# An RMSNorm and matmul kernel on one core: x tiles ahead of the weights, x buffers of 8, 16 and 16 tiles, finer stores at the end

## The chip, the core and the metric

The kernel runs on one core of a Trainium2 chip. The metric is the time of one execution on the device in microseconds (us), the median of several runs. A profile is one further execution with the hardware profiler on; its span, from the first to the last instruction, is some 1.8 us shorter than the time. An execution can be disturbed and then count as slow (over 1.5% above the fastest of its kernel); of a single run that cannot be told, so its state is called unknown. Ratios are the mean time of one kernel's fast runs over the mean of the other's fast runs of the same rounds, so they are not quite the ratios of the medians quoted.

## The reference

```python
def setup_inputs():
    batch, seq, dim, out_dim = 16, 1024, 512, 768
    # x: (16, 1024, 512) f32, gamma: (512,) f32, weight: (512, 768) f32, eps = 1e-5

def reference(x, gamma, weight, eps):
    rms = np.sqrt(np.mean(x ** 2, axis=-1, keepdims=True) + eps)
    x_norm = x / rms * gamma
    return np.matmul(x_norm, weight).astype(np.float32)
```

The 16,384 rows are 128 tiles of 128 rows. A tile is 0.262 MB of x in and 0.393 MB of output out.

## The kernel before

For each tile GpSimd casts x to bf16, TensorE transposes it as two float32 words (two transposes of 128x128), VectorE copies the transposes out of PSUM, TensorE multiplies by the weights (four products of 768 columns, each as 512 and 256), ScalarE squares x for the norm, and ScalarE and VectorE in turn scale the result by 1/rms on its way out. SyncE issues all loads and stores in one queue, in program order. gamma is multiplied into the weights once.

```python
    XG, OG = 16, 8
    AHEAD = 20
    ...
    opening = [1, 1, 1, 1, 2, 2]
    last = NT // OG - 1
    x_first, x_size = stretches(XG, {0: opening + [4, 4], 1: [4, 4, 8], 2: [8, 8]})
    o_first, o_size = stretches(OG, {0: opening, 1: [4, 4], last - 1: [4, 4], last: [2, 2, 1, 1, 1, 1]})
    ...
    xin = ctx.enter_context(tc.tile_pool(name="xin", bufs=2))       # two buffers of 16 tiles of x
    outp = ctx.enter_context(tc.tile_pool(name="out", bufs=3))      # three buffers of 8 tiles of output
    ...
        load_weights(0)          # first half of the weights
        load_until(3)            # x tiles 0, 1, 2
        load_weights(1)          # second half
        load_until(2 * XG)       # the rest of 32 tiles
    ...
        warm_up(6)               # idle matmuls
        ...                      # gamma turned by TensorE
        weights(0, nc.vector, 0, WIDE)
        weights(0, nc.vector, WIDE, O)
        weights(1, nc.scalar)
        warm_up(7)
        for i in range(3):
            cast(i, nc.gpsimd)
            square(i, ssq[:, i:i + 1])
        transpose_tile(0)
        transpose_tile(1)
        matmuls(0, acc[0], [0, 1])
        warm_up(3)
        transpose_tile(2)
        matmuls(1, acc[1], [0, 1])
        matmuls(2, acc[2], [0, 1])
        weights(2, nc.vector)    # needs the second half
        ...
        weights(3, nc.scalar)
        ...
        matmuls(0, acc[0], [2, 3])
        finish_tile(0, acc[0], nc.scalar)
    ...
        for j in range(2, NP):                       # pairs of tiles
            load_until(2 * j + AHEAD)
            ...                                      # cast of pair j + 3, squares and transposes of pair j + 2
            for i, engine in ((2 * j, nc.scalar), (2 * j + 1, nc.vector)):
                a = accumulator()
                matmuls(i, a, range(K), feed)
                finish_tile(i, a, engine)            # scales, and stores when a stretch is full
```

## Time and profile before

| | before |
|---|---|
| time, median of the first 3 runs | 210.98 us (210.57 to 211.02) |
| span of the profile | 209.0 us |
| TensorE busy | 201.6 us, 96% of the span |
| TensorE's last product ends | 203.1 us |
| last store issued, landed | 203.9 us, 208.0 us |
| moved | 85.7 MB, mean 410 GB/s |

Two answers of the profile belong together here. First, of the instructions of one line (the two stores of the last tile), how long from issue to landing, minimum, median and maximum:

```profile
DMA to landing us min/median/max: 4.1/4.1/4.1
```

Second, of the waits of SyncE's queue, the one at the program's end (waiter, releaser, total us, times, longest):

```profile
SPq L344 <- DMA out_dram<-ot: 3.5, 1, 3.5
```

So the program's last 3.5 us are a wait for stores that were all issued before. The lines of the opening and the sums over stretches stand in the prediction.

### The profile page before, as it was taken

The page shows a single profiled execution, that of the slowest core. Times are in us where ns is not written, and L with a number is a line of the kernel's source. Part 1 is how long each engine was busy: PE and PEld are TensorE (multiplying, and loading weights), DVE is VectorE, ACT ScalarE, POOL GpSimd, SP SyncE. Part 2 cuts the span into 40 slices and gives each one's busy share as a digit, 9 for nine tenths or more (in the row PEclk, how much of TensorE's full clock was granted, in tenths as well). Part 3 has the DMA queues.
Part 4 walks back from the last instruction along what each step waited for, and adds up shares of the span by engine and source line. Part 5 has one row for each costly group of instructions (what it writes and reads, how often), then busy time and mean ns, then how long its engine had stood idle before and what let it go on. Part 6 is the DMA issues. An engine that isn't in the chain of part 4 may idle for free.

```text
span 209.0 us, 3534 instructions
## 1 busy us (share of the span) xinstructions
PE 201.6 (96%) x1298; PEld 137.9 (66%) x1298; DVE 109.0 (52%) x173; ACT 149.6 (72%) x359; POOL 67.0 (32%) x73
## 2 busy tenths in 40 slices
PE   7999999999999999999999999999999999999980
PEld 2466777666766776667766776667667766677640
DVE  0465654654565465456545644654564465456550
ACT  2689987787778778777877777787777778777640
POOL 1357532306331073213623062310633045230000
PEclk9999999999999999999999999999999999999999
DMA  6999999999999999999999999999999999899994
GB/s 231 392 430 422 408 395 436 424 414 439 431 458 411 412 442 425 447 411 437 428 448 419 423 423 442 433 433 417 428 442 447 405 441 414 381 386 386 383 374 182
DMA packets 7077, 85.69 MB, mean 410 GB/s; under 512 B 786, under 2 KB 916, under 8 KB 3476
## 3 DMA queue, kind: packets, MB, share of 16 engines
q1 hardware_dynamic: 7056, 85.46, 97.0%
q8 instruction: 10, 0.16, 0.3%
q14 instruction: 7, 0.06, 0.1%
q10 hardware_dynamic: 4, 0.00, 0.0%
HBM read 35.13 MB, written 50.33 MB: 409 GB/s over the span
## 4 chain that ended last, share of the span: by engine, by line
PE 91%; ACT 3%; DMA 2%; POOL 1%; DVE 1%; issue 0%; SPq 0%
PE ops L168 77%; PE tp L133 13%; DMA xt<-in_x_dram 2%; ACT jk L98 1%; ACT ot L150 1%; POOL xb L94 1%; ACT rms L102 0%; DVE xT L140 0%; PE ops L227 0%; DVE ot L152 0%; SPq L206 0%; DVE rstd L104 0%
## 5 line engine op out<-in xcount | busy, mean ns | idle before, releaser
L168 PE MATMUL ops<-w_bf,xT 128*128 128x256 bf16 (+1 forms) x1024 | 194.2, 326 | 0.3 <-DVE xT L140 0.3
L168 PEld LDWEIGHTS <-xT 128*128 128x128 bf16 x1024 | 100.0, 98 | 56.4 <-DVE xT L140 1.4
L94 POOL CAST xb<-xt 128x1024 bf16<-128x1024 f32 (+1 forms) x67 | 66.3, 1002 | 118.9 <-PE tp L133 72.9
L150 ACT ACTIVATE ot<-ops,rstd 128x768 f32<-128x768 f32 (+1 forms) x65 | 58.1, 894 | 47.2 <-PE ops L168 47.2
L140 DVE COPY xT<-tp 128x1024 bf16<-128x1024 bf16 (+1 forms) x67 | 44.7, 667 | 83.3 <-PE tp L133 83.0
L98 ACT ACTIVATE jk<-xt 128x512 bf16<-128x512 f32 x128 | 78.7, 619 | 0.7 <-DMA xt<-in_x_dram 0.7
L133 PE MATMUL tp<-ident_f,xb 128*128 128x128 f32 x256 | 68.9, 273 | 0.1
L152 DVE TENSOR_SCALAR ot<-ops,rstd 128x768 f32<-128x768 f32 (+1 forms) x65 | 64.5, 993 | 2.9 <-PE ops L168 2.9
L133 PEld LDWEIGHTS tp<-ident_f,xb 128*128 128x128 f32 x256 | 35.9, 141 | 3.8 <-POOL xb L94 0.7
L98 ACT ACTIVATION_READ_ACCUMULATOR jk<-xt 128x1 f32 x128 | 24.4, 191 | 0.0
L102 ACT ACTIVATE rms<-ssq,eps_sb 128x4 f32<-128x4 f32 (+3 forms) x35 | 10.4, 297 | 1.1
L104 DVE RECIPROCAL rstd<-rms 128x4 f32<-128x4 f32 (+3 forms) x35 | 5.9, 167 | 3.3 <-ACT rms L102 3.3
L227 PE MATMUL ops<-warm 128*128 128x512 bf16 x16 | 6.4, 561 | 1.2 <-DVE eps_sb L220 1.2
L227 PEld LDWEIGHTS <-warm 128*128 128x128 bf16 x16 | 1.9, 131 | 3.9 <-issue 2.5
L150 ACT ACTIVATE w_bf<-w_f,g_sb 128x768 bf16<-128x768 f32 x2 | 1.9, 936 | 3.6 <-DMA w_f<-in_weight_dram 3.6
L201 ACT ACT_TABLE_LOAD x1 | 1.3, 1283 | 1.3 <-PEq L330 1.3
L152 DVE TENSOR_SCALAR w_bf<-w_f,g_sb 128x512 bf16<-128x512 f32 (+2 forms) x3 | 1.4, 485 | 1.1 <-DMA w_f<-in_weight_dram 1.0
L241 DVE COPY g_sb<-tp 128x4 f32<-128x4 f32 x1 | 0.2, 162 | 3.1 <-PE tp L239 3.1
L239 PEld LDWEIGHTS tp<-ident_f,g_row 2*128 2x128 f32 x2 | 0.3, 200 | 0.8 <-issue 0.8
L218 DVE MEMSET warm<- 128x256 uint32 x1 | 0.3, 272 | 0.9 <-PEq L330 0.9
L239 PE MATMUL tp<-ident_f,g_row 2*128 2x2 f32 x2 | 0.4, 264 | 0.0
masks.py:199 POOL TENSOR_SCALAR_AFFINE_SELECT ident_f<-ident_f 128x128 f32<-128x128 f32 x1 | 0.3, 292 | 0.1
(6 smaller groups left out, 0.7 us busy)
## 6 DMA issues: line engine op xcount, KB each, us to landing
out_dram<-ot SPq DMA_DIRECT2D x12, 3072.0 KB, 16.3
xt<-in_x_dram SPq DMA_DIRECT2D x5, 4096.0 KB, 23.0
xt<-in_x_dram SPq DMA_DIRECT2D x3, 2048.0 KB, 19.4
out_dram<-ot SPq DMA_DIRECT2D x4, 1536.0 KB, 11.6
xt<-in_x_dram SPq DMA_DIRECT2D x4, 1024.0 KB, 13.2
out_dram<-ot SPq DMA_DIRECT2D x4, 768.0 KB, 10.4
out_dram<-ot SPq DMA_DIRECT2D x7, 384.0 KB, 11.2
w_f<-in_weight_dram SPq DMA_DIRECT2D x2, 768.0 KB, 5.9
```

Of the source, the lines that this page charges most:

```text
L94: engine.tensor_copy(out=xb_tiles[i // 2][:, i % 2:i % 2 + n, :], in_=held(x_tiles, XG, i, n))
L98: nc.scalar.activation(out=jk, in_=held(x_tiles, XG, i)[:, 0, :], func=AF.Square, accum_out=ssq)
L102: nc.scalar.activation(out=rms[:, :n], in_=ssq[:, :n], func=AF.Sqrt, scale=1.0 / D, bias=eps_sb)
L104: nc.vector.reciprocal(out=rstd[:, :n], in_=rms[:, :n])
L133: nc.tensor.transpose(out=tp_tiles[j][:, t, h, :], in_=words[:, lo:lo + P], identity=ident_f)
L140: nc.vector.tensor_copy(out=dst[:, t:t + n, :], in_=src[:, t:t + n, :])
L150: nc.scalar.mul(out=dst, in_=src, mul=r)
L152: nc.vector.tensor_single_scalar(out=dst, in_=src, scalar=r, op=mybir.AluOpType.mult)
L168: nc.tensor.matmul(out=acc[:, lo:hi], lhsT=xT_tiles[i // 2][:, i % 2, k // 2, :, k % 2], rhs=w_bf[:, k, lo:hi], start=(k == 0), stop=(k == ...
L201: nc.scalar.preload_act_table(AF.Sqrt)
L227: nc.tensor.matmul(out=spare[:, :WIDE], lhsT=warm[:, :P], rhs=warm, start=True, stop=True)
L239: nc.tensor.transpose(out=gp[:, c, :], in_=g_row[:, :, c], identity=ident_f[:2, :2])
```

## The change

The intent is to have the first x tiles cast and transposed by the time the weights come, to read further ahead (40 tiles in place of 32), and to let the stores of the last 24 tiles start earlier in smaller pieces. The diff, cut to its core:

```diff
-    XG, OG = 16, 8
+    OG = 8
...
+    groups = [8] + [16] * 7 + [8]
+    base = [sum(groups[:g]) for g in range(len(groups))]
...
-    opening = [1, 1, 1, 1, 2, 2]
+    opening = [1, 2, 1, 2, 2]
...
-    x_first, x_size = stretches(XG, {0: opening + [4, 4], 1: [4, 4, 8], 2: [8, 8]})
-    o_first, o_size = stretches(OG, {0: opening, 1: [4, 4], last - 1: [4, 4], last: [2, 2, 1, 1, 1, 1]})
+    x_first, x_size = stretches(groups, {0: opening, 1: [4, 4, 8]})
+    o_first, o_size = stretches([OG] * (last + 1), {0: opening, 1: [4, 4], last - 2: [4, 4], last - 1: [2, 2, 2, 2],
+                                 last: [2, 2, 1, 1, 1, 1]})
...
+    xin_first = ctx.enter_context(tc.tile_pool(name="xin_first", bufs=1))
     xin = ctx.enter_context(tc.tile_pool(name="xin", bufs=2))
...
+        touched = singles.tile([P, 2, 1], F32)
+        nc.scalar.dma_start(out=touched, in_=wv[:, :, 0:1])
...
-        load_weights(0)
-        load_until(3)
-        load_weights(1)
-        load_until(2 * XG)
+        load_until(3)
+        for h in range(2):
+            nc.sync.dma_start(out=w_f32[:, 2 * h:2 * h + 2, :].rearrange("p c o -> p (c o)"), in_=wv[:, h, :])
+        load_until(base[3])
...
         warm_up(6)
+        cast(0, nc.vector)
+        square(0, ssq[:, 0:1])
...
+        transpose_tile(0)
+        warm_up(3)
+        cast(1, nc.vector)
+        cast(2, nc.gpsimd)
...
+        transpose_tile(1)
+        transpose_tile(2)
+        warm_up(6)
...
-        warm_up(7)
...
-        warm_up(3)
...
+        for k in (0, 1):
+            for i in range(3):
+                matmuls(i, acc[i], [k])
```

More of the change, by code (lines that the diff above doesn't have):

```diff
@@ L37, with stretches @@
     NP = NT // 2
-    XG, OG = 16, 8
+    OG = 8
     AHEAD = 20
     WIDE = 512
-    def stretches(group, parts):
+    groups = [8] + [16] * 7 + [8]
+    base = [sum(groups[:g]) for g in range(len(groups))]
+    group_of = [g for g, n in enumerate(groups) for _ in range(n)]
+    def stretches(sizes, parts):
         first, size, i = {}, {}, 0
-        for g in range(NT // group):
-            for n in parts.get(g, [group]):
+        for g, whole in enumerate(sizes):
+            for n in parts.get(g, [whole]):
                 for t in range(i, i + n):
@@ L53, in stretches @@
         return first, size
-    opening = [1, 1, 1, 1, 2, 2]
+    opening = [1, 2, 1, 2, 2]
     last = NT // OG - 1
-    x_first, x_size = stretches(XG, {0: opening + [4, 4], 1: [4, 4, 8], 2: [8, 8]})
-    o_first, o_size = stretches(OG, {0: opening, 1: [4, 4], last - 1: [4, 4], last: [2, 2, 1, 1, 1, 1]})
+    x_first, x_size = stretches(groups, {0: opening, 1: [4, 4, 8]})
+    o_first, o_size = stretches([OG] * (last + 1), {0: opening, 1: [4, 4], last - 2: [4, 4], last - 1: [2, 2, 2, 2],
+                                 last: [2, 2, 1, 1, 1, 1]})
     def rows(ap, i, n):
-        if i < XG:
+        g = group_of[i]
+        if g == 0:
             return ap[i * P:(i + n) * P, :].rearrange("(p t) d -> p t d", t=n)
-        return ap.rearrange("(g p t) d -> g p t d", p=P, t=XG)[i // XG, :, i % XG:i % XG + n, :]
+        whole = ap[base[g] * P:(base[g] + groups[g]) * P, :].rearrange("(p t) d -> p t d", t=groups[g])
+        return whole[:, i - base[g]:i - base[g] + n, :]
     singles = ctx.enter_context(tc.tile_pool(name="singles", bufs=1))
+    xin_first = ctx.enter_context(tc.tile_pool(name="xin_first", bufs=1))
     xin = ctx.enter_context(tc.tile_pool(name="xin", bufs=2))
@@ L75, with x_held, o_held @@
     x_tiles, xb_tiles, tp_tiles, rstd_of, xT_tiles, o_tiles, norm_sums = {}, {}, {}, {}, {}, {}, {}
-    def held(tiles, group, i, n=1):
-        return tiles[i // group][:, i % group:i % group + n, :]
+    def x_held(i, n=1):
+        g = group_of[i]
+        return x_tiles[g][:, i - base[g]:i - base[g] + n, :]
+    def o_held(i, n=1):
+        return o_tiles[i // OG][:, i % OG:i % OG + n, :]
     def load(i):
-        if i // XG not in x_tiles:
-            x_tiles[i // XG] = xin.tile([P, XG, D], F32, name="xt")
-        nc.sync.dma_start(out=held(x_tiles, XG, i, x_size[i]), in_=rows(x, i, x_size[i]))
+        g = group_of[i]
+        if g not in x_tiles:
+            x_tiles[g] = (xin if g else xin_first).tile([P, groups[g], D], F32, name="xt")
+        nc.sync.dma_start(out=x_held(i, x_size[i]), in_=rows(x, i, x_size[i]))
     starts = [i for i in range(NT) if x_first[i] == i]
@@ L93, in cast @@
             xb_tiles[i // 2] = xbp.tile([P, 2, D], BF16, name="xb")
-        engine.tensor_copy(out=xb_tiles[i // 2][:, i % 2:i % 2 + n, :], in_=held(x_tiles, XG, i, n))
+        engine.tensor_copy(out=xb_tiles[i // 2][:, i % 2:i % 2 + n, :], in_=x_held(i, n))
     def square(i, ssq):
         jk = junk.tile([P, D], BF16, name="jk")
-        nc.scalar.activation(out=jk, in_=held(x_tiles, XG, i)[:, 0, :], func=AF.Square, accum_out=ssq)
+        nc.scalar.activation(out=jk, in_=x_held(i)[:, 0, :], func=AF.Square, accum_out=ssq)
     def root(i, n, ssq):
@@ L164, in store @@
         if i == first + n - 1:
-            nc.sync.dma_start(out=rows(out, first, n), in_=held(o_tiles, OG, first, n))
+            nc.sync.dma_start(out=rows(out, first, n), in_=o_held(first, n))
     def matmul(i, k, acc, lo, hi):
@@ L200 @@
         nc.scalar.dma_start(out=g_row, in_=gamma.rearrange("(h w c) -> h w c", w=P, c=2))
+        wv = weight.rearrange("(h w c) o -> w h (c o)", w=P, c=2)
+        touched = singles.tile([P, 2, 1], F32)
+        nc.scalar.dma_start(out=touched, in_=wv[:, :, 0:1])
         nc.scalar.preload_act_table(AF.Sqrt)
-        wv = weight.rearrange("(h w c) o -> w h (c o)", w=P, c=2)
+        load_until(3)
         w_f32 = singles.tile([P, K, O], F32)
-        def load_weights(h):
+        for h in range(2):
             nc.sync.dma_start(out=w_f32[:, 2 * h:2 * h + 2, :].rearrange("p c o -> p (c o)"), in_=wv[:, h, :])
-        load_weights(0)
-        load_until(3)
-        load_weights(1)
-        load_until(2 * XG)
+        load_until(base[3])
         for _ in range(20):
@@ L241 @@
         nc.vector.tensor_copy(out=g_sb, in_=gp)
+        transpose_tile(0)
+        warm_up(3)
+        cast(1, nc.vector)
+        cast(2, nc.gpsimd)
+        square(1, ssq[:, 1:2])
+        square(2, ssq[:, 2:3])
+        transpose_tile(1)
+        transpose_tile(2)
+        warm_up(6)
         acc = [accumulator() for _ in range(4)]
@@ L245 @@
         weights(1, nc.scalar)
-        warm_up(7)
-        for i in range(3):
-            cast(i, nc.gpsimd)
-            square(i, ssq[:, i:i + 1])
-        transpose_tile(0)
-        transpose_tile(1)
-        matmuls(0, acc[0], [0, 1])
-        warm_up(3)
-        transpose_tile(2)
-        matmuls(1, acc[1], [0, 1])
-        matmuls(2, acc[2], [0, 1])
+        for k in (0, 1):
+            for i in range(3):
+                matmuls(i, acc[i], [k])
+        root(0, 3, ssq)
         weights(2, nc.vector)
-        root(0, 3, ssq)
         weights(3, nc.scalar)
@@ L262 @@
         finish_tile(0, acc[0], nc.scalar)
+        transpose_tile(3)
+        norms(3, 1)
         matmuls(1, acc[1], [2, 3])
-        transpose_tile(3)
         finish_tile(1, acc[1], nc.vector)
-        norms(3, 1)
         cast(4, nc.gpsimd)
```

## The prediction

> **What bounds the kernel now.** I read the page first (busy shares and slices), then the chain that ended last, then the waits of the engines and of the DMA queue, then sums over stretches, and last the timeline of the opening and of the tail.
>
> ```profile
> PE 201.6 (96%) x1298; PEld 137.9 (66%) x1298; DVE 109.0 (52%) x173; ACT 149.6 (72%) x359; POOL 67.0 (32%) x73
> ...
> GB/s 231 392 430 422 408 395 436 424 414 439 431 458 411 412 442 425 447 411 437 428 448 419 423 423 442 433 433 417 428 442 447 405 441 414 381 386 386 383 374 182
> ...
> PE 91%; ACT 3%; DMA 2%; POOL 1%; DVE 1%; issue 0%; SPq 0%
> ```
>
> TensorE is busy 96% of the span and is 91% of the chain, but the transfers run at over 400 GB/s in nearly every slice too. Two resources are nearly full at once. The sums over stretches show where TensorE is not full:
>
> ```profile
> 0.00:4.00 4.00, 2.81 (x8) 0.88 (x8) 0.28 (x2) 1.28 (x1) 0.70 (x6) 1.00 0.52 190
> 4.00:6.50 2.50, 2.50 (x8) 1.05 (x9) 0.91 (x3) 1.09 (x2) 0.49 (x1) 1.00 1.08 356
> 6.50:9.30 2.80, 2.72 (x16) 1.43 (x15) 0.85 (x2) 2.07 (x7) 1.36 (x3) 1.00 1.01 403
> 9.30:11.60 2.30, 2.30 (x15) 1.19 (x13) 1.13 (x3) 0.97 (x3) 0.61 (x1) 1.00 1.03 421
> 11.60:21.00 9.40, 9.13 (x61) 6.19 (x60) 5.87 (x12) 8.93 (x23) 6.39 (x8) 1.00 1.02 427
> 21.00:203.20 182.20, 182.14 (x1199) 127.17 (x1196) 99.52 (x152) 135.00 (x327) 57.45 (x56) 1.00 0.99 421
> 203.20:209.00 5.80, 0.00 (x0) 0.00 (x0) 0.46 (x1) 0.23 (x1) 0.00 (x0) 0.91 0.53 203
> ```
>
> The columns are the stretch, its length, busy time of TensorE, its weight loads, VectorE, ScalarE and GpSimd, then clock, DMA share, GB/s. From 21.0 to 203.2 TensorE idles 0.06 us in 182. In the timeline one tile takes 60.69 to 62.21 = 1.52 us there. One tile moves 0.262 MB in and 0.393 MB out, so TensorE's pace demands 0.655 MB / 1.52 us = 431 GB/s, which is about what the slices show. So only the first 11 us and the last 6 us can give anything; the middle gives nothing unless a wait appears in it. The opening hangs on the weights:
>
> ```profile
> 5.41 0.94 ACT L150 ACTIVATE w_bf<-w_f,g_sb 128x768 bf16<-128x768 f32 x1 [2.83 <-DMA w_f<-in_weight_dram]
> ...
> 8.24 0.61 POOL L94 CAST xb<-xt 128x512 bf16<-128x512 f32 x1 [0.98 <-DMA xt<-in_x_dram]
> ...
> 10.07 0.94 ACT L150 ACTIVATE w_bf<-w_f,g_sb 128x768 bf16<-128x768 f32 x1 [0.75 <-DMA w_f<-in_weight_dram]
> 10.07 0.62 DVE L152 TENSOR_SCALAR w_bf<-w_f,g_sb 128x768 bf16<-128x768 f32 x1
> ```
>
> The first weight half is there at 5.4 us, x tile 0 at 6.0, tile 2 at 8.2, the second half at 10.07; the scaled second half exists at 11.0, and tile 0 is finished at 11.59.
>
> **What the skill says.** (1) "DMA: Bandwidth & Descriptors", Specifications, gives a fabric ceiling of 435 GB/s and an HBM limit of about 358 GB/s per core. The trace agrees with the first (best long stretches about 430 GB/s) and contradicts the second (421 GB/s over 182 us). (2) The same page, Issuing engines are not separate DMA queues: transfers issued from several engines run on the same 16 engines and interleave. So the new transfer on ScalarE's queue takes its turn among those of x. (3) "TensorE: Matmul & The Clock Gate", Part 1, says that the array starts at half rate until a window of about 3.4 us was busy, and that the window is free-running. The trace agrees: idle matmuls start 0.43 us apart up to 6.3 us and 0.21 us apart at 8.4 us; its clock record steps up at 6.6 us.
>
> **The change part by part.**
>
> *Order of the first loads.* Before: weight half, three tiles, weight half. After: tile 0, tiles 1 and 2 in one transfer, both halves. Ahead of the last byte of the second half lie the same 2 x 0.786 + 3 x 0.262 = 2.36 MB. Scaling and the last two products of tiles 0 to 2 need that half, so its landing decides, and it moves only by efficiency: one transfer fewer to issue (about 0.5 us of queue time, but the engines are already fed), packets of 4 KB at 25.7 GB/s per engine in the trace where single tiles have 2 KB at 21.8 GB/s on average, slowed by a patch of poor packets at 4.5 to 6.5 us (313 to 357 GB/s). Restoring 400 GB/s in that patch saves about 0.4 us; the 256 four-byte pieces that touch the weights may cost some 0.1 us. I take 9.7 us for the landing in place of 10.04.
>
> *What TensorE can do before.* After, tile 0 may land at about 3.6 us, tiles 1 and 2 at 5, the first half at about 7.7. The six transposes (0.11 us each) are then out of the way. First half scaled on VectorE (0.48 + 0.27) and ScalarE (0.94): first product at about 8.3, and the twelve products (3 tiles x 2 x 0.32 us = 1.9 us) are done at 10.2. Then TensorE waits for the second half: 9.7 + 0.62 = 10.3 (VectorE), 9.7 + 0.94 = 10.65 (ScalarE); tile 0 ends at about 11.0, against 11.59. So the start is worth 0.5 us, not the 2 us by which tile 0 comes earlier.
>
> *Idle matmuls.* 6 + 3 + 6 = 15 against 16; they fill the wait for weights and cost nothing unless still at half rate: six at 0.43 are 2.6 us, from 6.3 to 8.9, which would push the first product 0.6 us but be absorbed by the wait for the second half (to about 0.3).
>
> *x buffers.* 8 tiles once, then 16 and 16: 40 tiles issued ahead instead of 32. Later a buffer of 16 is refilled when its last tile is squared, as before, only 8 tiles shifted. In the steady part the lead is unchanged. The last refill before took 22.9 us and was issued at 147.0; GpSimd waited 7.84 us for it and cast at 170.08, some 2 us ahead of TensorE's need. I expect the same lead. Early on, stores queue behind 2.1 MB more loads (4.9 us at 430 GB/s); tile 24's output buffer needs tiles 0 to 7 stored, about 37 us before, 42 after, and is asked for at 47. Hidden.
>
> *Tail.* Stores of 104 to 119 go from 8, 4, 4 tiles to 4, 4, 2, 2, 2, 2. The last eight tiles are stored as before. In the trace the last 13 or so of 16 engines pause at about 181, 193 and 199.7 us (0.4 to 1 us each) for want of a store, but three engines, some 5 us behind at 181, never pause and carry the last landing: stores issued from 199.2 on land 0.9 us apart up to 207.98. So filling the pauses helps the engines that don't matter. From the store at 196.2 on, the two programs have the same stores. Gain: 0 to 0.3 us, given back in part by smaller packets (6 KB against 12 and 24 KB: about 2% of 0.2 MB per engine at 26 GB/s, some 0.15 us).
>
> Sum: TensorE's end moves from 203.1 to about 202.6; of that the slow engines let through about 0.4 us. 210.98 - 0.4 - 0.1 = **210.5 us**.
>
> **The rivals.**
>
> *A. The tail is set by the queue, not TensorE.* For it: landings 0.9 us apart at the end. Then a start 0.5 us earlier is lost wholly in a longer queue: 211.0.
>
> *B. The pauses of the DMA engines in the tail count after all,* that is, the slow engines are slow through sharing and gain when stores come sooner; then the last landing comes 1 to 2 us sooner, 209 to 209.5. Against: their packets take the same 0.91 us while others pause.
>
> *C. A new wait in the middle:* the demand of 431 GB/s is all that the transfers give, so a load of 16 tiles coming 2 us later than the 2 us of lead would stall TensorE, perhaps twice: 212 to 214. Against: the lead in the steady part is worked out as unchanged, and in the early part grows to some 4 us.
>
> *D. The clock steps up later,* as the idle matmuls have gaps in which the array waits for tiles 0 to 2: up to 2 us of products at half rate, 1 us: 211.5.
>
> **Range and chances.** A and D push up by up to 1 us, B down by 1.5, and the start may be off by 0.4 either way. Range 209.3 to 211.5. Two per cent is 4.2 us: the ends that the trace shows hold only about 11 + 6 us in all, most of it needed for the first 2.4 MB and the last store, so faster by that needs things that I do not see (2%); slower needs C repeated (2%).
>
> **What would show it.** Right: second weight half landing at 9.4 to 10.1; first product at 8.0 to 9.0, tile 0 finished at about 11.0; TensorE idle under 0.5 us from 21 us to its end at about 202.6; tile pace 1.52 us; last landings still about 0.9 us apart with TensorE's end 4 to 5 us ahead of the span's. Wrong: a wait of the transposes for GpSimd's casts in the middle (C), products over 0.4 us long after 8.5 us (D), a span that ends under 5 us after TensorE (B), or one that does not move though TensorE ends sooner (A).

## The result and the profile after

In the same rounds the kernel before took 210.87 us (210.57 to 211.02, 6 runs) and the changed one 210.86 us (210.60 to 211.46, 6 runs). The ratio is 1.0003, with a 95% interval of 0.9988 to 1.0019: the same. The changed kernel's result is correct.

The opening came out at the times worked out (by what, is taken up below). From the timeline of the changed kernel (start, duration, engine, line, operation, what ended the idle time before):

```profile
7.55 0.94 ACT L163 ACTIVATE w_bf<-w_f,g_sb 128x768 bf16<-128x768 f32 x1 [1.38 <-DMA w_f<-in_weight_dram]
...
8.10 2.81 PE L181 MATMUL ops<-w_bf,xT 128*128 128x512 bf16 x16
...
9.37 0.94 ACT L163 ACTIVATE w_bf<-w_f,g_sb 128x768 bf16<-128x768 f32 x1 [0.70 <-DMA w_f<-in_weight_dram]
9.37 0.62 DVE L165 TENSOR_SCALAR w_bf<-w_f,g_sb 128x768 bf16<-128x768 f32 x1 [0.49 <-DMA w_f<-in_weight_dram]
...
10.95 0.90 ACT L163 ACTIVATE ot<-ops,rstd 128x768 f32<-128x768 f32 x1 [0.64 <-PE ops L181]
```

The second half of the weights is there at 9.37 us, not 10.07, and tile 0 is finished from 10.95, not 11.59. The gain is 0.64 us, and it is kept to TensorE's end, as the sums over stretches show (stretch, length, busy time of TensorE, its weight loads, VectorE, ScalarE, GpSimd, then clock, DMA share, GB/s):

```profile
180.00:190.00 10.00, 9.89 (x67) 7.03 (x67) 5.33 (x9) 6.97 (x18) 2.60 (x3) 1.00 0.99 418
190.00:202.50 12.50, 12.45 (x80) 8.00 (x78) 6.51 (x10) 7.47 (x16) 0.00 (x0) 1.00 0.88 359
202.50:209.00 6.50, 0.01 (x1) 0.00 (x0) 0.49 (x1) 0.30 (x1) 0.00 (x0) 0.90 0.49 188
```

TensorE ends at 202.5 (before: 203.1). In this trace 25 product records are missing, so the busy times of the first two rows are a little low; no wait is recorded there. But the same two views of the end as before read:

```profile
DMA to landing us min/median/max: 4.6/4.6/4.6
```

```profile
SPq L360 <- DMA out_dram<-ot: 3.9, 1, 3.9
```

The last store is issued 0.63 us sooner (203.25 against 203.88) and takes 0.5 us longer to land (4.58 against 4.10), so it lands 0.16 us sooner. What TensorE saved at the start was given back as a longer wait for stores at the end.

### The profile page after: what moved, and what is told of

Same layout as the page of the kernel before. It is cut to its first block, busy times and chain, and to the rows that moved or that the text cites. A ratio compares the mean times of both kernels' runs of the same rounds, so it can differ in the third digit from the quotient of the medians.

```text
span 208.8 us, 3508 instructions
## 1 busy us (share of the span) xinstructions
PE 199.8 (96%) x1272; PEld 138.1 (66%) x1297; DVE 109.9 (53%) x175; ACT 149.6 (72%) x359; POOL 65.5 (31%) x71
## 4 chain that ended last, share of the span: by engine, by line
PE 91%; DMA 3%; DVE 1%; ACT 1%; issue 1%; SPq 0%; DVEq 0%
PE ops L181 78%; PE tp L146 13%; DMA w_f<-in_weight_dram 3%; DVE ot L165 1%; ACT ot L163 0%; SPq L96 0%; ACT jk L111 0%; DVE w_bf L165 0%; DVE xT L153 0%; ACT rms L115 0%; DVE rstd L117 0%; DVEq L165 0%
## 5 line engine op out<-in xcount | busy, mean ns | idle before, releaser
L181 PE MATMUL ops<-w_bf,xT 128*128 128x512 bf16 (+1 forms) x999 | 192.5, 324 | 1.4
L107 POOL CAST xb<-xt 128x1024 bf16<-128x1024 f32 (+1 forms) x65 | 64.8, 1015 | 119.8 <-DMA xt<-in_x_dram 61.6
L239 PE MATMUL ops<-warm 128*128 128x512 bf16 x15 | 5.7, 530 | 1.2 <-DVE eps_sb L232 1.2
L107 DVE CAST xb<-xt 128x512 bf16<-128x512 f32 x2 | 0.9, 467 | 2.4 <-DMA xt<-in_x_dram 2.4
```

What stands on the lines that cost most here:

```text
L107: engine.tensor_copy(out=xb_tiles[i // 2][:, i % 2:i % 2 + n, :], in_=x_held(i, n))
L181: nc.tensor.matmul(out=acc[:, lo:hi], lhsT=xT_tiles[i // 2][:, i % 2, k // 2, :, k % 2], rhs=w_bf[:, k, lo:hi], start=(k == 0), stop=(k == ...
L239: nc.tensor.matmul(out=spare[:, :WIDE], lhsT=warm[:, :P], rhs=warm, start=True, stop=True)
```

## The experiments

Theory Q: the 16 transfer engines set the end. At least one of them has work queued from 2 us to the last landing, so TensorE has slack at its end, and moving TensorE moves nothing until the slack is used up. Rival P: TensorE sets the end, and a fixed landing follows it. All kernels below are variants of the changed one; unless said, they give the correct result. In the texts of what was expected, 210.86 us is the time of the changed kernel.

A table of what the profiles showed. "Weights" is the landing of the second half, "TensorE" the end of its last product, "issue" and "land" those of the last store that has a recorded landing:

| kernel | weights | TensorE | issue | land | landing less issue | time, median |
|---|---|---|---|---|---|---|
| before | 10.04 | 203.14 | 203.88 | 207.98 | 4.1 | 210.87 |
| changed | 9.35 | 202.51 | 203.25 | 207.82 | 4.6 | 210.86 |
| late_7 | 9.85 | 204.53 | 205.27 | 208.45 | 3.2 | 211.24 |
| late_19 | 8.75 | 206.69 | 207.43 | 210.08 | 2.7 | 212.46 |
| less_products | 9.07 | 197.32 | 199.01 | 208.26 | 9.2 | 210.74 |
| no_store_48 | 9.88 | 203.01 | 203.33 | 205.98 | 2.7 | 208.59 |
| old_start | 10.07 | 203.16 | 203.90 | 208.25 | 4.4 | 210.96 |
| old_tail | 9.89 | 203.05 | 203.79 | 208.27 | 4.5 | 210.69 |

### TensorE later: late_7 and late_19

```diff
         for j in range(2, NP):
...
+            if j == 30:
+                idle = accumulator()
+                for _ in range(7):        # 19 in late_19
+                    nc.tensor.matmul(out=idle[:, :WIDE], lhsT=warm[:, :P], rhs=warm, start=True, stop=True)
```

> The changed kernel with 7 idle matmuls (7 x 0.216 = 1.5 us of TensorE) put before tile 60. Theory Q (the transfers set the end; TensorE has slack at the end): the last store is issued 1.5 us later (about 204.8 in place of 203.25) but lands at about the same time as in the changed kernel (207.8), issue to landing shrinking from 4.6 to about 3.1 to 3.4 us; time 210.9 to 211.2. Rival P (TensorE's end plus a fixed landing sets the end): time 212.3, issue to landing still 4.6 us.

> The same with 19 idle matmuls (4.1 us). Theory Q: the slack is the 4.6 us from issue to landing less an unloaded landing of some 2.3 us (estimate from the first x tile, 2.7 us with its slow first packets), so about 2 us; beyond it the time follows TensorE: 210.86 + 4.1 - 2.1 = 212.9 us. Rival P: 215.0 us.

late_7 measured 211.24 us, ratio to the kernel before 1.0017 (1.0002 to 1.0032); late_19 212.46 us, ratio 1.0081 (1.0065 to 1.0097). In late_19's profile TensorE ended 4.2 us later than in the changed kernel's and the span grew by 2.3 us (211.1 against 208.8); the median time grew by 1.6 us, less than the 2.0 us expected. The issue to landing of the last store shrank, first in late_7, then in late_19:

```profile
DMA to landing us min/median/max: 3.2/3.2/3.2
```

```profile
DMA to landing us min/median/max: 2.7/2.7/2.7
```

Rival P wanted 212.3 and 215.0 us and a landing of 4.6 us in both. It falls. Where the queue has drained, a last store lands in 2.7 us, so of the changed kernel's 4.6 us some 1.9 us are queue: that is TensorE's slack. The completions of the last store, one from each of the 16 transfer engines, say the same: in the changed kernel they run from 205.69 to 207.82 us, in late_19 from 209.85 to 210.08. The lag of the slowest engine is gone there.

### TensorE sooner: less_products

The fourth product of tiles 108 to 123 is left out; the result is wrong. (The line that marks the last product of a sum is changed to match, and is cut here.)

```diff
...
         for k in ks:
+            if 108 <= i < 124 and k == K - 1:
+                feed and feed()
+                continue
             matmul(i, k, acc, 0, WIDE)
```

> The changed kernel with the fourth of the four products left out for tiles 108 to 123 (a wrong result on purpose): 16 x 0.32 = 5.1 us less on TensorE, every transfer kept. Theory Q: TensorE ends at about 197.4 in place of 202.5, the last landing stays within 0.5 us of 207.8, issue to landing of the last store grows from 4.6 to about 9.5 us; time 210.4 to 210.9. Rival P: time about 205.8 us.

The time was 210.74 us, ratio to the kernel before 0.9997 (0.9982 to 1.0012). TensorE ended 5.2 us sooner, and the last store landed 0.4 us later. The sums over stretches of this run say it in two rows:

```profile
190.00:197.40 7.40, 7.32 (x47) 4.43 (x44) 4.51 (x8) 3.90 (x9) 0.00 (x0) 1.00 1.01 421
197.40:209.30 11.90, 0.00 (x0) 0.00 (x0) 0.45 (x1) 0.21 (x1) 0.00 (x0) 0.67 0.55 220
```

TensorE has nothing to do for the last 11.9 us of this span, while 220 GB/s x 11.9 us = 2.6 MB are still moved, and the span is no shorter. A TensorE that is faster by 5 us is worth nothing here.

### Fewer bytes: no_store_48

The store of tiles 48 to 55 is left out (3.1 MB); the result is wrong.

```diff
-        if i == first + n - 1:
+        if i == first + n - 1 and first != 48:
```

> The changed kernel without the store of tiles 48 to 55 (3.1 MB, some 7.3 us of transfer; a wrong result on purpose), TensorE's work kept. Theory Q: the queue is empty at the end, the last store lands about 2.3 to 2.7 us after its issue in place of 4.6, time about 208.9 us; TensorE's end stays at 202.5. Rival P: no change, 210.9 us.

The time was 208.59 us, ratio 0.9887 (0.9866 to 0.9908). TensorE ended at 203.0 us, 0.5 us later than in the changed kernel's profile and not at the 202.5 expected, since the second half of the weights landed 0.5 us later (9.88 us). Its slices of GB/s (40 slices of the span) show the hole where the store is missing, and lower rates before the end than in the changed kernel (295 GB/s from 190 us to 203 against 359 from 190 us to 202.5):

```profile
GB/s 220 401 429 443 433 386 382 433 451 451 409 422 441 433 424 420 441 425 436 443 123 427 357 455 332 427 435 460 406 428 420 441 419 438 403 422 359 253 316 279
```

```profile
DMA to landing us min/median/max: 2.7/2.7/2.7
```

The hole is at about 104 us, 100 us ahead of the end, and takes 2.3 us off the time. 3.1 MB are some 7.3 us of transfer, but the gain stops where TensorE and the 2.7 us of an unloaded landing set the end. With the late runs this bounds the matter from both sides: the transfers are ahead of TensorE as the bound by about 2 us in 211, and a kernel whose queue has drained at the end would take about 208.6 us (an estimate: the median of this run) as long as TensorE ends where it does.

### The parts undone: old_start, old_tail, no_touch

old_start puts back the opening of the kernel before (order of loads, no touch, casts on GpSimd, its idle matmuls). old_tail puts back its stores of tiles 104 to 119. no_touch drops only the 256 four-byte reads.

```diff
 # old_tail
-    ... 1: [4, 4], last - 2: [4, 4], last - 1: [2, 2, 2, 2],
+    ... 1: [4, 4], last - 1: [4, 4],
                                  last: [2, 2, 1, 1, 1, 1]})
 # no_touch
-        touched = singles.tile([P, 2, 1], F32)
-        nc.scalar.dma_start(out=touched, in_=wv[:, :, 0:1])
```

> The changed kernel with the opening of the kernel before (first weight half, three x tiles, second half; no touch; casts on GpSimd); buffers and tail stay changed. Theory Q: TensorE's end goes back by about 0.6 us to 203.1, the time stays within 0.3 us of 210.9. Rival P (TensorE's end sets the time): +0.6 us against the changed kernel. Further, if the opening alone moves the second weight half, it lands at about 10.0 us again.

> The changed kernel with the stores of the kernel before in the tail (tiles 104 to 119 by 8, 4, 4). Theory Q with the slowest engines never pausing: the last landing stays within 0.3 us of 207.8, time 210.6 to 211.2. Rival B of the prediction (pauses of the other engines count): the last landing 0.5 us or more later.

> The changed kernel without the 256 four-byte reads of the weights. If the reads help, the first and second weight half land later than 7.46 and 9.35 us (by some 0.4 us, the patch of poor packets at 2.5 to 3.5 us returning later); if they only cost, earlier by 0.1 to 0.4 us. In either case the time stays at 210.9 within 0.4 us.

old_start: 210.96 us, ratio to the kernel before 1.0006 (0.9991 to 1.0021); its weights landed at 10.07 and TensorE ended at 203.16, back where the kernel before had them. old_tail: 210.69 us, ratio 0.9990 (0.9973 to 1.0007). Neither part moves the time by anything that these runs can tell from zero. In old_tail the last landing was 208.27 us, 0.45 us later than in the changed kernel's profile, between what the two theories wanted; but no_store_48 apart, last landings of kernels with the new tail reach 208.26 as well, so one profile does not decide this, and the times do not favour the new tail.

no_touch had its two halves at 8.00 and 9.93 us, time 210.83 us in its single run. Later than the changed kernel's 7.46 and 9.35, as if the touch helped; but late_7, no_store_48 and old_tail, which have the touch, show 9.85 to 9.89. Over the eleven profiles with the new order and the touch the second half was in use from 8.8 to 10.2 us. What the touch is worth stays open; it is within that spread, and hidden by the slack at the end.

### Do the 16 engines lag alike? probe_engines and probe_high

A transfer reports 16 completions, one for each engine, and the trace has their times. In the changed kernel the store of tiles 88 to 95 (issued at 143.96) reported its eighth completion at 162.01 us and its last three at 163.07, 164.71 and 164.75. So two engines run 2.7 us behind the middle one. The first lag is a small one from the start (0.8 us at 17 us). It stepped to 2.3 us between 17 and 22 us, when one 16 KB instruction fetch, at 21.4 us, took 1.10 us of some engine; a step of 0.7 to 1.6 us is at that time in 12 of the 14 profiles (not in no_touch and shift_4), but no run here removes the fetch, so its part in the lag is not shown. By 175 us the slowest is 4.2 us behind, and it catches up only while the others pause in the tail, to 2.1 us at the end. In less_products the last store's eighth completion came at 203.6 us and its last at 208.26: there too the middle engine was done 4.6 us before the last, and the late ones set the end.

To find which engines lag, the store of one tile was cut so that its pieces can use few engines. The Trainium skill, "DMA: Bandwidth & Descriptors", section Why a DMA increments its semaphore by 16 and not by 1, says that a store issued from SyncE uses the largest number of engines up to 16 that divides its slowest dimension, and the lowest-numbered ones. The trace agrees on the number: after one update of its semaphore (the counter that the engines raise) at its issue, a piece of n partitions of those up to 15 showed n more, and the piece of 84 partitions in probe_high showed 14. Which engines they are rests on the page alone.

```diff
...
+        if i == 96:
+            a = 0
+            for m in list(range(1, 16)) + [8]:        # probe_high: (8, 10, 12, 14, 84)
+                nc.sync.dma_start(out=rows(out, i, 1)[a:a + m, 0, :], in_=out_tile(i)[a:a + m, :])
+                a += m
...
```

(The stores of tiles 96 to 103 are split into 1 and 7 tiles for this. The expectations count the engines from 0, so their engine 4 is the fifth.)

> The changed kernel with the store of tile 96 cut into 15 stores of 1, 2, ... 15 partitions and one of 8, so that the store of n partitions can use n engines at most. If a few fixed engines lag by some 4 to 5 us (theory Q's slow engines), the landings go up in steps: small up to the number of the first slow engine, then a jump of 2 us or more, and flat after the slowest one. If the lag moves from engine to engine, or all lag alike, the landings rise evenly (some 0.1 to 0.3 us each). Time within 0.5 us of 210.9.

> The changed kernel with the store of tile 96 in pieces of 8, 10, 12, 14 and 84 partitions (on at most 8, 10, 12, 14 and 14 engines), followed by the 7 other tiles on 16. Every piece holds engine 4, so if engine 4 is a fixed slow one, each of the pieces ends with one landing some 3 to 4 us after the others; a second late landing that first appears in the n-th piece tells of a second slow engine among those added. If the slow engine changes from run to run, the piece of 8 may show none. Time 210.9 within 0.5 us, as five stores do not fill the queue as sixteen did.

The pieces of 1, 2, 3, 4, 5, 6 and 7 partitions had their last completions at 167.95, 169.34, 169.56, 169.79, 173.18, 173.37 and 173.56 us. The jump of 3.4 us comes with the fifth piece, and the other completions of the later pieces stayed below 170.6. So in this run one engine, the fifth, was behind, and the first four, the sixth and the seventh were not. The probe spoiled its own second half: the program has eight completion semaphores in turn, with eight stores unlanded SyncE issued nothing more from 165.7 to 173.0 us, and by then the lag was gone; the load queued behind came late, and the run (a single one, state unknown) took 217.36 us instead of the expected 211. In probe_high (212.55 us in its single run, again more than expected) the piece of 8 partitions had completions from 167.89 to 173.92 us, the last one 2.7 us after the one before it. That agrees with the fifth engine but tells no number. One more can be read there: the whole store before the pieces had two late completions, at 173.48 and 173.69 us; the pieces of 8, 10 and 12 partitions have only one completion after 173.48, the piece of 14 has two (173.63 and 174.53). So, by the same numbering, the second late engine of that run is the thirteenth or the fourteenth.

### Bytes moved off the late engine: shift_4, shift_8, shift_16

If a late engine among numbers 5 to 16 sets the end, giving part of its bytes to the first four should shorten the run.

```diff
-            nc.sync.dma_start(out=rows(out, first, n), in_=o_held(first, n))
+            cuts = [(0, 112), (112, 116), (116, 120), (120, 124), (124, 128)] if first == 48 else [(0, P)]
+            for lo, hi in cuts:
+                nc.sync.dma_start(out=rows(out, first, n)[lo:hi], in_=o_held(first, n)[lo:hi])
```

(shift_4 has stores of 4 tiles at 48 to 55 and cuts the first; shift_16 cuts those at 48 and 64.)

> The changed kernel with one store of 8 tiles (48 to 55) cut into one of 112 partitions (7 for each of 16 engines) and four of 4 partitions (24 KB to each of engines 0 to 3 alone). Engines 0 to 3 get 4 x 0.91 - 0.91 = 2.7 us more to move, each of the others 0.91 us less. Theory Q, with the end set by a slow engine that is not among 0 to 3 (the first probe found engine 4 some 4 us behind, 0 to 3 and 5, 6 not): the last landing comes about 0.9 us sooner (206.9 in place of 207.8 to 208.2), since engines 0 to 3 take most of their 2.7 us out of pauses in the tail; time about 210.0. If the end were set by all engines alike, or by TensorE: 210.9 or above.

> The same with a store of 4 tiles cut: engines 0 to 3 get 1.4 us more, the others 0.46 us less. Theory Q: last landing about 0.45 us sooner, time about 210.4. Otherwise 210.9.

> The same with two stores of 8 tiles cut: engines 0 to 3 get 5.5 us more, the others 1.8 us less. Theory Q: engines 0 to 3 now are the slow ones: four engines instead of one to three lag in the tail, the last landing at about 208.5 to 209.3; time 211.4 to 212.2. If no fixed engine sets the end: 210.9.

All three are correct and far slower: shift_4 215.69 us (ratio 1.0226, 1.0213 to 1.0239), shift_8 221.05 us (1.0479, 1.0454 to 1.0503), shift_16 227.10 us (1.0745, 1.0709 to 1.0780). The expectation of 210.0 to 212.2 was wrong, and not by a wrong theory of the end alone: the pieces cost several times what I gave them. The stretches of shift_8:

```profile
90.00:108.00 18.00, 17.90 (x118) 12.67 (x120) 9.95 (x15) 13.40 (x34) 4.16 (x4) 1.00 1.01 432
108.00:120.00 12.00, 11.95 (x80) 8.38 (x80) 6.64 (x10) 8.78 (x22) 6.13 (x6) 1.00 1.02 320
120.00:135.00 15.00, 9.68 (x49) 6.00 (x48) 3.65 (x6) 5.67 (x13) 2.08 (x2) 0.77 0.98 386
```

From 108 us, when the pieces reach the engines, all engines stay busy (share 1.02) but move 320 GB/s in place of 432: packets of 24 KB took up to 5.1 us each, against 0.91 us in the changed kernel, where none in this stretch took over 1.32. The pieces' completions came at 115 to 127 us. Only then was their output buffer free again, and TensorE waited for ScalarE, which was to write into it. From the timeline of shift_8:

```profile
127.16 0.90 ACT L163 ACTIVATE ot<-ops,rstd 128x768 f32<-128x768 f32 x1 [7.90 <-DMA out_dram<-ot]
...
128.11 0.59 PE L183 MATMUL ops<-w_bf,xT 128*128 128x512 bf16 x1 [5.26 <-ACT ot L163]
```

That is the idle time of the last row of the stretches above. Later TensorE waited 1.5 us (to 146.1) and 0.9 us (to 171.5) for casts of x tiles, the first of which had come late, and its granted clock was half from 126.2 to 133.1 us, hence the 0.77 in that row. The eight semaphores had no part in this: from 95 to 153 us SyncE's last wait before a transfer was for VectorE, ScalarE or GpSimd, never for a landing. Why packets of so few partitions are so slow no run here shows. So the shift does not test whether the fifth engine sets the end, and the kernel that was to beat both does not. How to even out the engines stays open.

## Why the prediction was right or wrong

Right in its numbers, step by step, though not each for the reason given:

- **The opening.** The second half was expected at 9.7 us and landed at 9.35; the first product at 8.3, it was 8.10; tile 0 finished at 11.0, it was 10.95; TensorE's end at 202.6, it was 202.51. Much of this is luck. The prediction had the second half sooner by better packets ahead of it; but the eighth of its 16 completions came at 8.54 us in both profiles, before and after, and only the last moved, from 10.04 to 9.35. Over all 14 profiles the eighth lies between 8.44 and 8.76 us and the last between 8.75 and 10.12. So the landing was set by how far one to three engines lagged in that profile. The two profiles with the old order have 10.04 and 10.07 us, the eleven with the new order and the touch 8.75 to 10.12; that the order moves it is not shown. That x tile 0 comes 2.5 us sooner (3.47 against 5.96) was worth no more than the second half of the weights let through.
- **Idle matmuls.** They cost nothing in this profile: the last ended at 8.04 us, and the first scaled weights were there at 8.05. The clock stepped up at 6.35 us, before the first product, and between 4.0 and 7.0 us in the other profiles, so rival D did not come about.
- **Buffers.** TensorE shows no wait from 21 us on. GpSimd waited up to 8.2 us for a load and, after one wait of 8.1 us, cast from 157.56, again some 2 us ahead of TensorE's need, as worked out. Rival C did not come about. No run undid the buffers alone.
- **Tail.** Finer stores gained nothing that the times show: old_tail was 210.69 us. Why the pauses of the other engines did not count is argued from the trace and from less_products, whose end stayed though its stores came 5 us sooner; it was not isolated by a run of its own. The slow engines of the kernel before were less far behind than the prediction had it: at 181 us the last completion came 3.8 us after the middle one, not 5.

Wrong in size: the step that "of that the slow engines let through about 0.4 us" of TensorE's gain. The runs show a slack of 1.9 us between TensorE and the end (4.6 us less the 2.7 us of an unloaded landing), so that all of it was swallowed. The times agree: the ratio forecast, 210.5 / 210.98 = 0.9977, lies outside the measured interval (0.9988 to 1.0019). Rival A, which gave 211.0 us, described what happened; I had put it down as an upward risk and should have made it the centre, since the landings 0.9 us apart at the end and the issue to landing of 4.1 us were in view. Also wrong was one sign named in advance, that the span ends 4 to 5 us after TensorE: it is 6.3 us, and even before it was 5.8; I had confused it with the landing time of the last store. The prediction's range held because every one of these terms is small against the 211 us.

## What to carry to other kernels

When two resources are both nearly full (here TensorE for 96% of the span, the transfer engines for 97%), ask which of them still has work queued when the other has finished: the issue to landing time of the last stores, put against that of an unloaded one, gives the slack of the engine that looks like the bound. Here a gain in the opening of that engine was lost in the drain at the end, and so is any other until the slack is gone. A transfer lands with the slowest of its engines, so look at all its completions before a landing is explained by order or size. Test it from both sides before you tune: make the compute shorter (nothing happened), leave out a transfer in the middle (2.3 us came off at once), and only then decide what to shorten.

## What the Trainium skill lacked or had wrong

- "DMA: Bandwidth & Descriptors", Latency and other measured facts: names engines 7 and 15, counted from 0, as usually slower and ties this to descriptor rings of the GpSimd path. Here all bulk transfers are issued by SyncE, and the late engines that could be placed were, counted from 0, engine 4 (3.2 us behind the others of its piece at 173.18 us) and engine 12 or 13.
- No page gives how far engines with equal bytes drift apart: in the nine profiles other than the probes and the shifts, the last of 16 completions came 0.2 to 1.5 us after the middle one at 9 us, and 2.3 to 4.8 us after it near 174 us.
